# Strassen's scheme for the gate and up products of 1792 tokens: an encoder layer on one core, cut into two phases

## The chip, the core and the metric

The kernel runs on one core of one Trainium2 chip. The core has four compute engines with a queue each: TensorE (PE; PEld is its weight load), VectorE (DVE), ScalarE (ACT) and GpSimd (POOL). SyncE (SP) issues the DMA transfers. The engines run side by side and meet at semaphores. The metric is the time of one launch on the device, in microseconds (us); lower is better.

## What is computed

The reference is one layer of an encoder over 2048 prompt tokens and 32 sample tokens with state, D_MODEL = 1024:

```python
h = layer_norm(x, ln_in_g, ln_in_b)
m, states = mixer(h, ...)       # z = h @ w_in (1024 x 2304), three mixers on z, then @ w_out
h = layer_norm(ALPHA * h + m, ln1_g, ln1_b)
f = swiglu(h, w_gate, w_up, w_down)
h = layer_norm(ALPHA * h + f, ln2_g, ln2_b)

def swiglu(h, w_gate, w_up, w_down):     # 1024 x 2816, 1024 x 2816, 2816 x 1024
    a = jnp.einsum('btd,df->btf', h, w_gate)
    b = jnp.einsum('btd,df->btf', h, w_up)
    return jnp.einsum('btf,fd->btd', jax.nn.silu(a) * b, w_down)
```

The mixers are A (convolution of width 4 and a gated linear recurrence), B (retention in chunks of 64) and C (attention over a window of 128). All is float32.

## The kernel before

**Products.** Each large product of float32 values is made of three products in a reduced float32 format: every operand is split into a high and a low part, and high x high, low x high and high x low are added up in PSUM. A weight tile arrives in `stage` by DMA (`feed`, L172); ScalarE copies it to `whi` (`first_part`, L177), VectorE subtracts that from `stage` to give `wlo` (`second_part`, L182). `product` (L727) makes 24 matmuls of a unit, 3 x 8 slices of 128 of the 1024 features, the weights being the stationary side and the tokens the columns that stream. The columns of the normalized rows are held as hA (before the mixers) and hB (before the gate), high and low.

**Blocks.** The tokens are cut in blocks of 256, 384, 384, 384, 384 and 256, with the sample's 32 in the first one (288 columns). Per block there are units of four kinds:
- W: 18 units, the input projection, each 24 matmuls; results leave through ScalarE to the mixers' buffers.
- O: 8 units, the output projection. Here tokens are stationary and 512 weight columns stream (`t_unit`, L811 to L813; the sample's part L819); `accumulate` adds to the rows in `tok` (L837, L839).
- G: 44 units, gate and up of each of 22 feature tiles of 128 (`gu_unit`). Of a gate unit ScalarE takes tanh (L782) and VectorE forms silu (L783); of an up unit VectorE multiplies (L788), ScalarE copies the high part g_h (L789), VectorE subtracts for g_l (L794).
- D: the down projection of a group of feature tiles, added to the rows. The groups are tiles 0 to 5, 6 to 11, 12 to 17 and 18 to 21. A D unit holds two feature tiles; a group's products begin with its first two.

**Order.** `seq` is written out by hand: the G and D units of a block are followed by W of the block two further on, with O of the next block between its feature tiles 17 and 18. What is not a unit (the mixers, LayerNorms, transposes) runs as side threads, Python generators: before each unit `step` lets threads go on as far as a credit allows that grows by `rate` a unit (twice a unit where "twice" is set). The mixers of block b + 1 run through the G units of block b. Before each unit `feed` issues DMA loads as far as four `stage` buffers allow, and `split` has the parts of the next units made. The order in which the program calls the engines is the order on each engine's queue.

LayerNorm (`norm`) takes statistics on VectorE (L290), normalizes on ScalarE (L298), multiplies on VectorE (L300) and adds on GpSimd (L302); `to_features` transposes rows on TensorE. `last` (L1030 to L1064) ends the program token tile by token tile.

Of the kernel before, what the change touches and what calls it, by code (L numbers as in the profile page):

```python
# [15 lines left out]
D = 1024  # L16
# [16 lines left out]
START = tuple(int(x) for x in np.cumsum((0,) + BLOCKS[:-1]))  # L33
# [12 lines left out]
# Column offsets of the tables that depend on shapes alone.  # L46
# [37 lines left out]
def tile_hybrid_step(ctx: ExitStack, tc: tile.TileContext, io, outs):  # L84
# [4 lines left out]
    sb = ctx.enter_context(tc.tile_pool(name="sb", bufs=1))  # L89
    ps = ctx.enter_context(tc.tile_pool(name="ps", bufs=1, space=bass.MemoryType.PSUM))  # L90
    ctx.enter_context(tc.manual_schedule())

# [6 lines left out]
    # ---------------------------------------------------------------- blocks  # L99
    def ptok(b):  # L100
        return BLOCKS[b]

    def ncol(b):
        return BLOCKS[b] + (DEC if b == 0 else 0)

    def ttiles(b):
        t = [(i * 128, 128) for i in range(BLOCKS[b] // 128)]
        return t + ([(BLOCKS[b], DEC)] if b == 0 else [])

    # ---------------------------------------------------------------- token rows  # L110
    tok = {}

    def load_x(b, ts=(0, 1, 2)):
        for t, (c0, rows) in enumerate(ttiles(b)):
            if t not in ts:
                continue
            x = sb.tile([128, D], F32, name="tok", bufs=9)
# [4 lines left out]
            tok.setdefault(b, []).append(x)  # L122

    load_x(0, (0,))
    head = cst.tile([128, 144], F32, name="head")
    ident = head[:, :128]
    g_in, b_in = head[:, 128:136], head[:, 136:144]
    tb = cst.tile([128, TB_W], F32, name="tb")
    sm = cst.tile([128, SM_W], F32, name="sm")
# [5 lines left out]
    # Products of zeros wake the tensor engine's clock.  # L135
    busy = sb.tile([128, 512], F32, name="bc", bufs=2)
# [20 lines left out]
    # ---------------------------------------------------------------- weights  # L157
# [4 lines left out]
    def raw(u):  # L162
        """Whether the unit's own values are read by the tensor engine too."""
# [27 lines left out]
    # ---------------------------------------------------------------- side work  # L191
# [10 lines left out]
    def advance(name):  # L202
        """The thread's next stage; about how much work for the vector engine it is."""
# [9 lines left out]
    def step():  # L213
        """Some side work: a stage of each thread whose turn it is, while there is time for it."""
# [12 lines left out]
    def pipeline(gens, every):  # L227
        """Generators one after the other, each starting some stages after the last."""
# [34 lines left out]
    # ---------------------------------------------------------------- layer norms  # L263
    def bcast(name):
        t = sb.tile([128, D], F32, name="bc", bufs=2)
# [4 lines left out]
    def norm(name, b, g, be):  # L270
        """LayerNorm of the block's rows, in place."""
        while norming:
            yield
        norming.append(name)
        gt, bt = bcast(g), bcast(be)
        st = sb.tile([128, 3, 2, 6], F32, name="ln_st", bufs=2)
        mv = sb.tile([128, 3, 2], F32, name="ln_mv", bufs=2)
        rs = sb.tile([128, 3], F32, name="ln_rs", bufs=2)
# [27 lines left out]
        if name == "n1":  # L306
            # The first block's rows, of which only the columns have had them.
# [3 lines left out]
    def to_features(b, hi, lo):  # L311
        """Rows to feature-major columns, each value as two float32r parts."""
# [13 lines left out]
    def hl(b, tag):  # L326
        n = ncol(b)
        return (sb.tile([128, 8, n], F32R, name=tag + "h"), sb.tile([128, 8, n], F32R, name=tag + "l"))

    hA, hO, hB = {}, {}, {}  # L330
# [8 lines left out]
    def ln1(b):  # L339
        yield from norm(f"m{b}", b, "ln1_g", "ln1_b")  # L340

    def h1(b):
        hB[b] = hl(b, "hB")
        yield from to_features(b, *hB[b])

    def ln1_h1(b):
        yield from ln1(b)
        yield from h1(b)

    def ln2(b):  # L350
        yield from norm(f"y{b}", b, "ln2_g", "ln2_b")
        for t, (c0, rows) in enumerate(ttiles(b)):
            if c0 < BLOCKS[b]:
# [4 lines left out]
        del tok[b]  # L358

    # ---------------------------------------------------------------- persistent state of the mixers  # L360
    kb = cst.tile([128, 512], F32, name="kb")
    ks = S("ck")
    axtail = cst.tile([128, 2, 3], F32, name="axtail")
    lru = cst.tile([128, 2], F32, name="lru")
    ret = cst.tile([128, 2, 128], F32, name="ret")
    ret_s = S("ret").rearrange("p (t e) -> p t e", t=2)
    lam = cst.tile([128, 8, 2], F32, name="lam")
    hb = cst.tile([128, 2, 2], F32, name="hb")
    SBUFS = {}
    for kv in range(2):  # L370
        SBUFS["e", kv] = cst.tile([128, 2, 193], F32, name=f"sbe{kv}")
        SBUFS["o", kv] = cst.tile([128, 2, 257], F32, name=f"sbo{kv}")
# [6 lines left out]
    def prepare(b):  # L379
        """-4 and 2 softplus(-lambda), and half the gates' biases."""  # L380
# [861 lines left out]
```

## Time and profile before

| | |
|---|---|
| median of 3 runs | 2348.68 us (2348.56 to 2350.0) |
| span of the profiled execution | 2347.9 us |
| PE busy | 2319.7 us, 99%, 13755 matmuls |
| DVE busy | 1494.9 us, 64% |
| ACT busy | 1012.5 us, 43% |
| POOL busy | 283.9 us, 12% |
| DMA | 328.42 MB, 140 GB/s |

The profile is one execution recorded by the hardware. A row of the groups has line, engine, operation, output and inputs, shapes and count; then busy time in us and mean ns of one; then the idle time of the engine ahead of these instructions and the work that ended it. A row of the timeline has start and duration in us; what stands in brackets is idle time before the instruction and what ended it. A matmul's duration in the timeline contains its way through the array, so the pitch of a run of matmuls is read from start to start.

### The profile page before, as it was taken

What the parts mean: (1) busy time and instruction counts of PE and PEld (TensorE: products, weight loads), DVE (VectorE), ACT (ScalarE), POOL (GpSimd) and SP (SyncE); (2) the same over time, 40 slices, a digit from 0 to 9 for tenths busy, and PEclk for the clock granted to TensorE, in tenths of its full rate; (3) what the DMA queues carried; (4) which work ended last, traced back from release to release, by engine and by line L of the source; (5) the groups of instructions that cost most, each with busy time, mean ns of one, the idle gap of its engine ahead of it and who ended that gap; (6) DMA issues with size and microseconds to landing.
All of it is one profiled execution on the core that took longest, in us unless ns stands there. A gap on an engine that the chain in (4) does not pass through costs nothing. (4 is left out here: it accounts for less than half of the span.)

```text
span 2347.9 us, 34907 instructions
## 1 busy us (share of the span) xinstructions
PE 2319.7 (99%) x13755; PEld 2106.4 (90%) x13755; DVE 1494.9 (64%) x2401; ACT 1012.5 (43%) x1662; POOL 283.9 (12%) x321
## 2 busy tenths in 40 slices
PE   9899999999999999999999999999999999999998
PEld 7789888789988989998898999899899988989997
DVE  8666877583766548466664755666477565457656
ACT  5534555343543424444443434444344434334443
POOL 4112321031110002111000120100013000001001
PEclk9999999999999999999999999999999999999999
DMA  6225434444432334443233354233345323344654
GB/s 227 99 94 200 140 119 143 146 168 157 147 112 100 113 123 141 171 157 111 102 110 123 135 173 153 106 108 108 126 137 211 122 99 119 127 169 153 209 186 153
DMA packets 91907, 328.42 MB, mean 140 GB/s; under 512 B 11488, under 2 KB 12320, under 8 KB 91744
## 3 DMA queue, kind: packets, MB, share of 16 engines
q1 hardware_dynamic: 91744, 326.20, 40.0%
q8 instruction: 108, 1.77, 0.3%
q14 instruction: 55, 0.45, 0.1%
HBM read 317.34 MB, written 8.82 MB: 139 GB/s over the span
## 5 line engine op out<-in xcount | busy, mean ns | idle before, releaser
L182 DVE TENSOR_TENSOR wlo<-stage,whi 128x1024 fp32r<-128x1024 f32 x549 | 729.1, 1329 | 373.0 <-PE mm L813 122.7
L177 ACT ACTIVATE whi<-stage 128x1024 fp32r<-128x1024 f32 x551 | 580.7, 1054 | 446.7 <-PE mm L812 329.9
L727 PE MATMUL mm<-hBh,whi 128*128 128x384 f32 (+2 forms) x2112 | 388.5, 325 | 0.0
L727 PE MATMUL mm<-hBh,wlo 128*128 128x384 f32 (+2 forms) x2112 | 376.1, 319 | 3.9 <-DVE wlo L182 3.8
L727 PE MATMUL mm<-hBl,whi 128*128 128x384 f32 (+2 forms) x2112 | 376.1, 319 | 0.0
L727 PEld LDWEIGHTS mm<-hBh,whi 128*128 128x128 f32 x2112 | 337.5, 189 | 14.8 <-issue 8.5
L727 PEld LDWEIGHTS mm<-hBh,wlo 128*128 128x128 f32 x2112 | 341.1, 188 | 4.8 <-DVE wlo L182 4.8
L727 PEld LDWEIGHTS mm<-hBl,whi 128*128 128x128 f32 x2112 | 341.3, 188 | 0.0
L811 PE MATMUL mm<-whi,g_h 128*128 128x512 f32 x688 | 277.2, 403 | 0.1
L813 PE MATMUL mm<-wlo,g_h 128*128 128x512 f32 x688 | 272.7, 396 | 0.0
L812 PE MATMUL mm<-whi,g_l 128*128 128x512 f32 x688 | 271.3, 394 | 0.0
L789 ACT ACTIVATE g_h<-g_t 128x384 fp32r<-128x384 f32 (+2 forms) x132 | 65.4, 495 | 351.6 <-DVE g_t L788 351.6
L783 DVE SCALAR_TENSOR_TENSOR g_t<-g_t,mm 128x384 f32<-128x384 f32 (+2 forms) x132 | 67.9, 514 | 192.5 <-ACT g_t L782 191.9
L788 DVE SCALAR_TENSOR_TENSOR g_t<-g_t,mm 128x384 f32<-128x384 f32 (+2 forms) x132 | 67.9, 514 | 162.4 <-PE mm L727 162.0
L727 PE MATMUL mm<-hAh,wlo 128*128 128x384 f32 (+2 forms) x864 | 157.0, 324 | 7.0 <-DVE wlo L182 7.0
L811 PEld LDWEIGHTS mm<-whi,g_h 128*128 128x128 f32 x688 | 129.2, 188 | 38.5 <-issue 7.8
L782 ACT ACTIVATE g_t<-mm 128x384 f32<-128x384 f32 (+2 forms) x132 | 60.6, 459 | 233.6 <-PE mm L727 233.5
L727 PE MATMUL mm<-hAh,whi 128*128 128x384 f32 (+2 forms) x864 | 157.8, 324 | 1.0 <-DVE zb L939 0.5
L813 PEld LDWEIGHTS mm<-wlo,g_h 128*128 128x128 f32 x688 | 129.2, 188 | 31.5 <-DVE wlo L182 0.4
L727 PE MATMUL mm<-hAl,whi 128*128 128x384 f32 (+2 forms) x864 | 155.5, 322 | 0.0
L812 PEld LDWEIGHTS mm<-whi,g_l 128*128 128x128 f32 x688 | 129.3, 188 | 28.9
L295 POOL TENSOR_TENSOR ln_rs<-ln_rs,mhalf 128x1 f32<-128x1 f32 (+1 forms) x46 | 36.8, 799 | 944.9 <-DVE ln_mv L293 944.9
(273 smaller groups left out, 2691.1 us busy)
## 6 DMA issues: line engine op xcount, KB each, us to landing
stage<-in_wgu SPq DMA_DIRECT2D x264, 512.0 KB, 3.5
stage<-in_wdn SPq DMA_DIRECT2D x132, 512.0 KB, 3.5
stage<-in_win SPq DMA_DIRECT2D x108, 512.0 KB, 3.5
stage<-in_wout SPq DMA_DIRECT2D x48, 512.0 KB, 3.5
tok<-in_x SPq DMA_DIRECT2D x16, 512.0 KB, 6.0
out_y<-tok SPq DMA_DIRECT2D x14, 512.0 KB, 5.4
bc<-in_ln_g SPq DMA_DIRECT2D x12, 512.0 KB, 5.4
bc<-in_ln_b SPq DMA_DIRECT2D x12, 512.0 KB, 6.2
```

The lines of the kernel that those rows point to most:

```text
L177: act.activation(whi[u], staged[u], AF.Copy)
L182: eng.tensor_tensor(wlo[u], staged[u], whi[u].bitcast(F32), op=ALU.subtract)
L295: pool.tensor_tensor(rs[:rows, t:t + 1], rs[:rows, t:t + 1], mhalf[:rows, 0:1], op=ALU.pow)
L727: pe.matmul(p, w[:, k, :], a[:, k, :], start=(x == 0 and k == 0), stop=(x == 2 and k == 7))
L782: act.activation(t, p[:, :N], AF.Tanh, scale=0.5)
L783: dve.scalar_tensor_tensor(t, t, 1.0, p[:, :N], op0=ALU.add, op1=ALU.mult)
L788: dve.scalar_tensor_tensor(t, t, 0.5, p[:, :N], op0=ALU.mult, op1=ALU.mult)
L789: act.activation(gh, t, AF.Copy)
L811: pe.matmul(o, ah[:, cs], wh[:, x, :], start=first and x == 0, stop=False)
L812: pe.matmul(o, al[:, cs], wh[:, x, :], start=False, stop=False)
L813: pe.matmul(o, ah[:, cs], wl[:, x, :], start=False, stop=last and x == 1)
```

## The change

The program falls into two phases.

**Phase 1** has W and O of all blocks, the mixers and the first two LayerNorms, and the whole SwiGLU of block 0 alone (at its end, groups of four feature tiles). W of block b + 1 is followed by O of block b; the mixers of a block run beside the W and O units of its neighbours, with rate 1.8 and two steps a unit. The rows after the second LayerNorm go to DRAM, and so do their transposes (`to_memory`, instead of the split into hB).

**Phase 2** has the SwiGLU of the other 1792 tokens. Phase 1's buffers in SBUF and PSUM are given up and new ones opened in their place. The tokens form two parts of 896, each of two halves of 448. In a part, for each feature tile, gate and up form a product of a 2 x 2 block matrix of the columns (halves of tokens by halves of features, 448 x 512) with a 2 x 2 block matrix of the weights (halves of features by gate and up). Strassen's scheme, in Winograd's form, makes it of 7 block products for 8, each of 3 x 4 matmuls of 448 columns. The operands are sums of blocks: those of the columns are made once a part (`columns`: 14 copies on ScalarE, 14 subtractions and 8 sums of 896 on VectorE), those of the weights for every feature tile (sums on GpSimd, copies on ScalarE, subtractions on VectorE, tiles of 512). The gate and up values are sums of products, formed by `after_p1` to `after_p3` when a product leaves PSUM.

Weight work is a list of jobs, of which `background(3)` does up to three behind each product; seven pairs of high and low parts and six unsplit tiles are held. `down` is the down projection of a group of three (twice two) feature tiles over the seven token tiles of the part; `finale` the last one with the last LayerNorm.

```diff
-GROUPS = ((0, 6), (6, 12), (12, 18), (18, 22))
+GROUPS0 = ((0, 4), (4, 8), (8, 12), (12, 16), (16, 20), (20, 22))
+GROUPSS = ((0, 3), (3, 6), (6, 9), (9, 12), (12, 15), (15, 17), (17, 19), (19, 22))
+HALF = 448
+PART = 2 * HALF
+NPAIR = 7
+NRAW = 6
...
+    phase.close()
+    phase = ctx.enter_context(ExitStack())
+    sb = phase.enter_context(tc.tile_pool(name="ff", bufs=1))
+    ps = phase.enter_context(tc.tile_pool(name="pf", bufs=1, space=bass.MemoryType.PSUM))
...
+            for x, th, kh in (("a", 0, 0), ("d", 0, 1), ("c", 1, 1), ("b", 1, 0)):
+                w[x] = two()
+                sp.dma_start(w[x], cols1[s, th, kh][:, k, :])
...
+        def multiply(n, left, right, first):
+            if first:
+                bank[n] = gbank()
+            (wl, wh), = need([(s, f, right)])
+            xl, xh = X[left]
+            for x, (w, a) in enumerate(((wh, xh), (wl, xh), (wh, xl))):
+                for k in range(4):
+                    pe.matmul(bank[n], w[:, k * 128:k * 128 + 128], a[:, k, :],
+                              start=first and x == 0 and k == 0,
+                              stop=x == 2 and k == 3, skip_group_check=not first)
+            drop([(s, f, right)])
...
+        def after_p3():
+            t = GT[f] = sb.tile([128, 2, PART], F32R, name="g", bufs=3)
+            dve.tensor_tensor(v["u2"], v["u2"], bank["z"], op=ALU.add)
+            dve.scalar_tensor_tensor(v["u2"], v["g1"], 0.5, v["u2"], op0=ALU.mult, op1=ALU.mult)
+            dve.scalar_tensor_tensor(v["g2"], v["g2"], 1.0, v["c"], op0=ALU.add, op1=ALU.mult)
+            act.activation(t[:, 1, :HALF], v["u2"], AF.Copy)
+            dve.scalar_tensor_tensor(v["p5"], v["g2"], 0.5, v["p5"], op0=ALU.mult, op1=ALU.mult)
+            act.activation(t[:, 1, HALF:], v["p5"], AF.Copy)
+
+        def low():
+            t = GT[f]
+            dve.tensor_tensor(t[:, 0, :], v["raw"].rearrange("p a b -> p (a b)"), t[:, 1, :].bitcast(F32),
+                              op=ALU.subtract)
...
+        for n, left, right, first, then in (
+                ("x", "a11", "b11", True, after_p1), ("z", "s1", "t1", True, after_p5),
+                ("y", "s2", "t2", True, after_p6), ("x", "a12", "b21", False, after_p2),
+                ("v", "a22", "t4", True, after_p4), ("y", "s3", "t3", False, after_p7),
+                ("z", "s4", "b22", False, after_p3)):
+            multiply(n, left, right, first)
+            catch_up()
+            behind(then)
+            background(3)
+            step()
+        behind(low)
...
+    def down(s, g, more=None):
+
+        fs = list(range(*GROUPSS[g]))
+        catch_up()
+        for half in range(2):
+            need([(s, f, half) for f in fs])
+            banks_ = {}
+            if half == 0:
+                for t in range(2):
+                    banks_[t] = dbank()
+                    d_part(s, half, t, fs[:-1], banks_[t], True, False)
```

`catch_up` calls what `behind` put off, so a product's results leave PSUM behind the next product; before `down`, those of the last product of a group are called ahead of its matmuls.

Three places in the queues. On SP before, in the middle of the program, weight loads wait only for the buffer that they overwrite (`in_wdn` is the down weights, `in_wgu` gate and up; the bracket names the engine or DMA queue waited for):

```order
L172 DMA stage<-in_wdn 128x1024 [waits DMAHW1_49,DVE_49]
L172 DMA stage<-in_wgu 128x1024 [waits DMAHW2_49,DVE_49,Activation_49]
L172 DMA stage<-in_wgu 128x1024 [waits DMAHW3_49,DVE_49]
L172 DMA stage<-in_wgu 128x1024 [waits DMAHW4_49,DVE_49]
L172 DMA stage<-in_wgu 128x1024 [waits DMAHW5_49,DVE_49]
```

On SP now, where phase 1 ends (`stage` is its last weights) and phase 2 begins (`ww` its weight tiles, `cols` the columns in DRAM):

```order
L206 DMA stage<-in_wdn 128x1024 [waits DMAHW2_49,PE_49]
L206 DMA stage<-in_wdn 128x1024 [waits DMAHW4_49,DVE_49]
L1190 DMA ww<-in_wgu 128x512 [waits DMAHW5_49,DMAHW0_49,DMAHW6_49,DVE_49,DMAHW7_49,PE_49,Pool_49]
L1190 DMA ww<-in_wgu 128x512 x5
L1153 DMA two<-cols_75 128x896
L1153 DMA two<-cols_76 128x896
L1153 DMA two<-cols_78 128x896 [waits DMAHW1_49]
```

The first load of phase 2 waits for every engine, for TensorE's last product among them (L909), and all loads behind it stand in the same queue.

On TensorE before, where the down products of a group follow on its last gate and up unit (mm is a bank of PSUM, g_h and g_l the parts of a feature tile's result):

```order
L727 MATMUL mm<-hBh,whi 128x384 x7
L727 MATMUL mm<-hBh,wlo 128x384 x8
L727 MATMUL mm<-hBl,whi 128x384 x8
L811 MATMUL mm<-whi,g_h 128x512 [waits Activation_49]
L812 MATMUL mm<-whi,g_l 128x512
L813 MATMUL mm<-wlo,g_h 128x512 [waits DVE_49]
```

And now, the end of a group's last seventh product, the products of the tiles that are ready, and the first of the last tile (gu and dn are banks, g both parts of a result):

```order
L1323 MATMUL gu<-xh,wl 128x448 x4
L1323 MATMUL gu<-xl,wh 128x448 x4
L1386 MATMUL dn<-wh,g 128x512
L1387 MATMUL dn<-wh,g 128x512
L1388 MATMUL dn<-wl,g 128x512
...
L1386 MATMUL dn<-wh,g 128x512 [waits Activation_49]
L1387 MATMUL dn<-wh,g 128x512 [waits DVE_49]
L1388 MATMUL dn<-wl,g 128x512
```

The waits of the down products stood behind the first two of six tiles' weights; they stand now behind 12 matmuls of the last tile's two neighbours, and wait for that last tile. On VectorE, at the same place, now:

```order
L1351 TENSOR_TENSOR two<-two,gu 128x448 [waits DVE_49,PE_49]
L1352 TENSOR_TENSOR two<-two,gu 128x448 [waits DVE_49]
L1203 TENSOR_TENSOR wl<-ww,wh 128x512 [waits DMAHW1_49,Activation_49]
L1358 TENSOR_TENSOR two<-two,gu 128x448 [waits PE_49]
L1359 SCALAR_TENSOR_TENSOR two<-two 128x448 [waits DVE_49]
L1360 SCALAR_TENSOR_TENSOR two<-two 128x448
L1362 SCALAR_TENSOR_TENSOR two<-two 128x448 [waits DVE_49,Pool_49]
L1367 TENSOR_TENSOR g<-two,g 128x896 [waits Activation_49]
L1393 SCALAR_TENSOR_TENSOR tok<-tok,dn 128x512 [waits DMAHW0_49,PE_49]
```

A weight's subtraction (L1203, waiting for ScalarE's copy) stands ahead of the four operations on the seventh product and of the subtraction that gives the low part (L1367).

More of the change, by code (lines that the diff above doesn't have):

```diff
@@ L785, in gu_unit @@
             t = gate_bank.pop(f)
-            gh = sb.tile([128, N], F32R, name="g_h", bufs=6)
-            gl = sb.tile([128, N], F32R, name="g_l", bufs=6)
+            f0, f1 = next(g for g in GROUPS0 if g[0] <= f < g[1])
+            if f == f0:
+                g_parts[0] = hl(b, "hC", 4, 2)
+            gh, gl = (x[:, f - f0, :] for x in g_parts[0])
             dve.scalar_tensor_tensor(t, t, 0.5, p[:, :N], op0=ALU.mult, op1=ALU.mult)
@@ new lines, in weights_d, with loads @@
+    def weights_d(s, g, half):
+        f0, f1 = GROUPSS[g]
+        for f in range(f0, f1):
+            w_load((s, f, half), io["wdn"][half * (FT // 2) + f // 2][:, (f % 2) * 512:(f % 2) * 512 + 512])
+        for f in range(f0, f1):
+            w_hi((s, f, half), (s, f, half))
+            w_lo((s, f, half), (s, f, half), True)
+    def loads():
+        while clock["next"] < len(jobs) and (jobs[clock["next"]][0] != "load" or clock["raw"] < NRAW):
+            kind, fn, _ = jobs[clock["next"]]
+            if kind == "load":
+                fn()
+            clock["next"] += 1
@@ new lines, in job, with background @@
+    def job():
+        kind, fn, _ = jobs[clock["done"]]
+        if kind == "pair" and clock["pairs"] == NPAIR:
+            return False
+        if kind != "load":
+            fn()
+        clock["done"] += 1
+        return True
+    def background(n):
+        clock["slot"] += 1
+        loads()
+        while n and clock["done"] < clock["next"]:
+            kind, _, on = jobs[clock["done"]]
+            if any(landed.get(k, 0) > clock["slot"] for k in on) or not job():
+                break
+            n -= kind != "load"
@@ new lines, in need, with drop @@
+    def need(keys):
+        for k in keys:
+            while clock["done"] <= ends[k]:
+                loads()
+                assert clock["done"] < clock["next"] and job(), k
+        return [pairs[k] for k in keys]
+    def drop(keys):
+        for k in keys:
+            del pairs[k]
+            clock["pairs"] -= 1
+    ends = {}
+    for s_ in range(NPART):
+        for g_, (f0_, f1_) in enumerate(GROUPSS):
+            for f_ in range(f0_, f1_):
+                weights_gu(s_, f_)
+            for half_ in range(2):
+                weights_d(s_, g_, half_)
@@ new lines, in d_part, with d_add @@
+    def d_part(s, half, t, fs, bank, first, last):
+        for f in fs:
+            wl, wh = pairs[s, f, half]
+            gl, gh = (GT[f][:, i, t * 128:t * 128 + 128] for i in range(2))
+            pe.matmul(bank, gh, wh, start=first and f == fs[0], stop=False)
+            pe.matmul(bank, gl, wh, start=False, stop=False)
+            pe.matmul(bank, gh, wl, start=False, stop=last and f == fs[-1])
+    def d_add(s, half, t, bank, fresh):
+        r = tok[NBLK + s][t][:, half * 512:half * 512 + 512]
+        if fresh:
+            dve.scalar_tensor_tensor(r, r, ALPHA, bank, op0=ALU.mult, op1=ALU.add)
+        else:
+            dve.tensor_tensor(r, r, bank, op=ALU.add)
@@ new lines, in down @@
+    def down(s, g, more=None):
[8 more added lines that the diff above has]
+                    d_part(s, half, t, fs[:-1], banks_[t], True, False)
+            for t in range(PART // 128):
+                if t in banks_:
+                    d_part(s, half, t, fs[-1:], banks_[t], False, True)
+                else:
+                    banks_[t] = dbank()
+                    d_part(s, half, t, fs, banks_[t], True, True)
+                catch_up()
+                behind(lambda t=t, b=banks_[t], half=half: d_add(s, half, t, b, g == 0))
+                if more:
+                    next(more, None)
+                background(3)
+                step()
+            drop([(s, f, half) for f in fs])
@@ new lines, in finale @@
+        normal(t, c2)
+        whole(t, c0)
+        affine(t, c2, pool, pool)
+        whole(t, c1)
+    pace.update(rate=1.0, credit=0.0, twice=False)
+    start("y0", ln2(0))
+    loads()
+    for _ in columns(0):
+        background(2)
+    for s_ in range(NPART):
+        for g_, (f0_, f1_) in enumerate(GROUPSS):
+            for f_ in range(f0_, f1_):
+                gu(s_, f_)
+            if g_ == 0:
+                drain("y0" if s_ == 0 else f"y{NBLK + s_ - 1}")
+            if g_ < len(GROUPSS) - 1:
+                down(s_, g_)
+            elif s_ < NPART - 1:
+                more_ = columns(s_ + 1)
+                down(s_, g_, more_)
+                catch_up()
+                for _ in more_:
+                    pass
+                start(f"y{NBLK + s_}", ln2(NBLK + s_))
+            else:
+                finale(s_, g_)
```

553 lines of the change are left out of this document (368 added, 185 removed).

## The prediction

> **What bounds the kernel now.** I read the head of the page first, then the waits of TensorE, then the timeline for the pitch of its products.
>
> ```profile
> span 2347.9 us, 34907 instructions
> PE 2319.7 (99%) x13755; PEld 2106.4 (90%) x13755; DVE 1494.9 (64%) x2401; ACT 1012.5 (43%) x1662; POOL 283.9 (12%) x321
> PEclk9999999999999999999999999999999999999999
> ```
>
> ```profile
> engine line waited for: us in total, times, longest us
> PE mm L727 <- DVE wlo L182: 10.9, 6, 6.3
> PE mm L919 <- ACT tok L914: 2.6, 2, 1.9
> ```
>
> TensorE is busy 99% of the span and its longest class of waits is 10.9 us. So the time is the number of matmuls times their pitch, and two things can move it: fewer columns to stream, or TensorE made to wait where it does not wait now.
>
> The pitch is read from where one product's group of eight starts to where the next starts (the columns are start, duration, line, tile):
>
> ```profile
> 1001.69 1.55 PE L727 MATMUL mm<-hAl,whi 128*128 128x384 f32 x8
> 1003.07 1.55 PE L727 MATMUL mm<-hAh,whi 128*128 128x384 f32 x8
> ...
> 2203.66 1.12 PE L727 MATMUL mm<-hBh,whi 128*128 128x256 f32 x8
> 2204.62 1.12 PE L727 MATMUL mm<-hBh,wlo 128*128 128x256 f32 x8
> ...
> 2330.18 0.40 PE L1030 MATMUL mm<-whi,g_h 128*128 128x512 f32 x1
> ...
> 2331.81 0.39 PE L1031 MATMUL mm<-hAh,g_l 128*128 128x512 f32 x1
> ```
>
> With the rest of the timeline (8 to a row, and 7 between the last two) that is 1.387/8 = 173 ns for 384 columns, 0.963/8 = 120 ns for 256 and 1.63/7 = 233 ns for 512.
>
> **The change, part by part.** The sum is made against the profiled span, 2347.9 us; the median of the runs is 2348.7, 0.8 above it, and I leave that difference alone.
>
> *Gate and up products.* Before, the 1792 tokens behind block 0 take 44 units of 24 matmuls in each of four blocks of 384 and one of 256: 4224 x 0.1734 + 1056 x 0.120 = 732 + 127 = 859 us. After, 22 feature tiles x 2 parts x 7 products x 12 = 3696 matmuls of 448. No row has 448: per column 384 gives 202 ns, 512 gives 204; I take 203. 3696 x 0.203 = 750 us, so **-109 us** (-105 to -112). Down, output and input products and block 0 keep their matmuls, so this is the whole gain. All else is waiting.
>
> The costs need the durations of the other engines:
>
> ```profile
> L182 DVE TENSOR_TENSOR wlo<-stage,whi 128x1024 fp32r<-128x1024 f32 x549 | 729.1, 1329 | 373.0 <-PE mm L813 122.7 <-PE mm L727 118.4 <-issue 101.8
> L839 DVE TENSOR_TENSOR tok<-tok,mm 128x512 f32<-128x512 f32 x92 | 63.2, 688 | 40.5 <-PE mm L813 39.9
> L290 DVE BATCH_NORM_STATS2 ln_st<-tok 128x6 f32<-128x512 f32 x88 | 56.2, 680 | 0.0
> L783 DVE SCALAR_TENSOR_TENSOR g_t<-g_t,mm 128x384 f32<-128x384 f32 x88 | 48.7, 554 | 150.6 <-ACT g_t L782 150.0
> L789 ACT ACTIVATE g_h<-g_t 128x384 fp32r<-128x384 f32 x88 | 46.3, 526 | 259.5 <-DVE g_t L788 259.5
> L319 ACT ACTIVATE hBh<-sd 128x512 fp32r<-128x512 f32 x30 | 15.9, 587 | 0.1
> L302 POOL TENSOR_TENSOR tok<-tok,bc 128x1024 f32<-128x1024 f32 x44 | 110.6, 2515 | 198.4 <-DVE tok L300 197.1 <-DVE lam L396 1.3
> ```
>
> Between these shapes I interpolate: VectorE 0.62 us for 448 and 1.10 for 896 (between 0.688 at 512 and 1.23 for an L182 that runs alone, quoted below), ScalarE 0.57 for 448 and 0.59 for 512, GpSimd half of 2.5 for 512, 1.26.
>
> *The step between the phases.* The first weight and column loads of phase 2 stand on SP's queue behind a wait for the last product of phase 1 (the new pools reuse its memory), so nothing of phase 2 is prepared while phase 1 computes. A load of this size takes, from issue to landing (last column, us):
>
> ```profile
> stage<-in_wgu SPq DMA_DIRECT2D x264, 512.0 KB, 3.5
> ```
>
> Six weight loads of 256 KB and four of 0.46 MB come at once: 3.4 MB against 3.5 us for half a MB; I estimate 7 us (4 to 11) until VectorE has its first operands. It then has, in its order up to the operand of the seventh product, 22 operations of 896 and 8 of 512: 22 x 1.10 + 8 x 0.69 = 30 us, less some 2 for overlap at their ends. ScalarE's 14 + 8 copies (about 18 us) run beside it. The seventh product (12 x 0.203 = 2.4 us) follows, and ends at 7 + 28 + 2.4 = 37 us, where TensorE's own work is 84 x 0.203 = 17: 20 us too late. Loads of the second slice wait for buffers, and GpSimd's sums interfere (below), for which I choose 10 more: **+30 us** (18 to 42). And TensorE is cold after that:
>
> ```profile
> 64.56 2.29 PE L727 MATMUL mm<-hAh,wlo 128*128 128x288 f32 x8 [6.32 <-DVE wlo L182]
> 66.64 2.12 PE L727 MATMUL mm<-hAl,whi 128*128 128x288 f32 x8
> ...
> 70.05 1.34 PE L727 MATMUL mm<-hAh,whi 128*128 128x288 f32 x8
> 71.23 1.21 PE L727 MATMUL mm<-hAh,wlo 128*128 128x288 f32 x8
> ```
>
> After a wait of 6.32 us eight matmuls of 288 took 2.08 us, a little later 1.18: some 4 us at about half speed, so **+2 us**. The Trainium skill, "TensorE: Matmul & The Clock Gate", section "What's actually happening", says that the clock is halved after an idle window of some 3.4 us and restored after a busy one; these rows agree. That page speaks against each shorter wait below as well, if it passes that length; this is a rival.
>
> *Entry into the down products.* Before, the last gate product's chain is hidden under down products of other feature tiles. After, a group has only 3 tiles (2 in two of the eight groups), and its products start with the tiles that are ready (6 or 12 matmuls of 512 for two token tiles), then need the last tile. Its chain hangs on the seventh product: the scalar copy of a weight into the buffer that this product releases and VectorE's subtraction of it stand ahead in the two queues (0.59 + 0.69), then four operations of 448 (2.48), a copy (0.57), a subtraction of 896 (1.10), and hand-offs. From a product's end to the start of the vector operation, and from there to ScalarE's copy:
>
> ```profile
> 2326.50 0.39 PE L1030 MATMUL mm<-whi,g_h 128*128 128x512 f32 x1
> ...
> 2326.70 0.42 DVE L788 SCALAR_TENSOR_TENSOR g_t<-g_t,mm 128x256 f32<-128x256 f32 x1 [0.84 <-PE mm L727]
> ...
> 2327.16 0.42 ACT L789 ACTIVATE g_h<-g_t 128x256 fp32r<-128x256 f32 x1 [1.94 <-DVE g_t L788]
> ```
>
> it is 0.20 us, counted from when the next product begins; and 2326.70 + 0.42 to 2327.16 is 0.04; with 0.04 for each of four hand-offs, 5.8 us in all. Cover is 13 matmuls (3.0 us) or 7 (1.6), so TensorE waits 2.8 or 4.2 us: 11 x 2.8 + 4 x 4.2 + 4.2 for the last group = **+52 us** (25 to 68; without the weight's pair ahead it is 1.28 less each time, some 32, and one more operation ahead gives 16 more).
>
> *Where part 0 ends.* The second part's columns are made between the last down products of the first: VectorE then has 22 x 1.10 + 14 x 0.69 for residuals and 6 x 0.69 for weights = 38 us, TensorE 126 x 0.233 = 29, but the columns of the later products have another 17 us of gate products to come in: **+7** (0 to 14).
>
> *The end.* Each of the last seven token tiles takes 18 x 0.233 = 4.2 us of TensorE and on VectorE two additions (1.38), four statistics of 256 (1.7 by half of L290 and an overhead), two multiplications (1.38) and half a us of small ones: 5.0. 7 x 0.8 = **+6** (3 to 13).
>
> *Phase 1.* The mixers of a block, spread before over input, output, gate and down products, now run beside input and output products alone:
>
> ```profile
> 50.00:150.00 100.00, 91.95 (x635) 83.70 (x634) 71.73 (x169) 51.83 (x118) 16.80 (x21) 0.97 0.29 97
> 150.00:350.00 200.00, 199.07 (x1330) 172.31 (x1328) 146.53 (x252) 100.32 (x172) 46.77 (x47) 1.00 0.42 147
> 1040.00:1400.00 360.00, 360.00 (x1983) 325.60 (x1982) 223.70 (x349) 149.99 (x244) 37.78 (x42) 1.00 0.36 125
> ```
>
> The columns are stretch, length, then busy time (and count) of PE, PEld, DVE, ACT and POOL, and the granted clock. VectorE is 62% busy at 1040 to 1400, 73% at 150 to 350. Counting its operations in the new order by these durations gives 77 to 88 us a block beside some 95 to 115 of TensorE, about 80%. At 73% TensorE lost under 1 us in 200; in the prologue, where mixers already run so beside input products, it lost 8 in 100. Five blocks of some 105 us between these two: **+13** (-5 to 42; a gain only from side products that now fall into waits that stand there anyway).
>
> *GpSimd's sums.* Each feature tile has four weight sums and one sum of products on GpSimd, 5 x about 1.26 us, which the kernel before does not have. These rows show what that does to a vector operation with two operands in SBUF:
>
> ```profile
> 203.81 2.40 POOL L302 TENSOR_TENSOR tok<-tok,bc 128x1024 f32<-128x1024 f32 x1 [2.30 <-DVE tok L300]
> 204.99 2.29 DVE L182 TENSOR_TENSOR wlo<-stage,whi 128x1024 fp32r<-128x1024 f32 x1 [1.26 <-ACT tok L298]
> ...
> 213.31 1.23 DVE L182 TENSOR_TENSOR wlo<-stage,whi 128x1024 fp32r<-128x1024 f32 x1 [1.35 <-PE mm L727]
> ```
>
> The subtraction, 1.23 alone, takes 2.29 and ends 1.07 after GpSimd's: it stood until GpSimd was done. The Trainium skill, "SBUF — State Buffer", section "Who interferes with whom", has the two engines share a port pair under an exclusive lock; the rows agree. In a feature tile's 17 us VectorE has 7 x 0.69 + 8 x 0.62 + 1.10 = 11 us; five full blockings would make it 17. Half of that is likelier, since GpSimd's sums meet other operations too. Weights are split several products ahead and results have two banks' time, which covers a blocking here and there: **+6** (0 to 44, a us per tile, if not).
>
> Sum: 2347.9 - 109 + 32 + 52 + 7 + 6 + 13 + 6 = 2355 us.
>
> **The rivals.** *The waits are cheap* (0.27). Phase 1 goes as 150 to 350 went, at no cost, the boundary and the end cost 4 each, the sums nothing, and the entries lose only what lies without the weight's pair ahead, 32: 2347.9 - 109 + 32 + 32 + 8 = 2311 us, faster. For it: TensorE's 199.07 of 200 at 73%. Against it: the weight's copy waits for the very product that starts the chain. It decides if an entry costs under 2 us.
>
> *VectorE binds phase 1* (0.16). Each of the five blocks loses as the prologue did and as much again when threads must be finished: 9 us x 5 = 45 instead of 13, 2387 us. For it: 91.95 of 100. Against it: 6.3 us of that were one wait. It decides if VectorE is over 90% busy there.
>
> *The entries cool the clock* (0.05): if each of 15 waits of 3 to 4 us brings the half speed seen after 6.32, 2 us each, 2385 us. Against it: they are shorter than the wait shown.
>
> *The lock binds phase 2* (0.04): a us in each of 44 tiles instead of 6 in all, 2393 us.
>
> *The change doesn't do what it says* (0.02): if matmuls of 448 took the 233 ns of 512, 3696 x 0.233 = 861 us and the gain is gone, 2355 + 111 = 2466 us.
>
> **How the numbers follow.** The forecast has 0.46, with its own range of 2338 to 2372; the measurement can tell about 0.2%, 2344 to 2353.4. Of the 0.46 I put 0.12 below that, 0.15 inside, 0.19 above. Faster: 0.27 + 0.12 = 0.39; same 0.15; slower 0.19 + 0.16 + 0.05 + 0.04 + 0.02 = 0.46. The range of 8 in 10 begins at 2311, which leaves half of the first rival (0.13) out, and ends at 2400, which leaves the last rival and some 0.05 of the others out.
>
> **What would show it.** Right: one wait of TensorE of some 25 to 40 us in all around the step between the phases, with PEclk down after it; 15 waits of 2.5 to 4.5 us ending at VectorE's subtraction of 896 (L1367); matmuls of 448 at 203 ns; phase 1 with VectorE near 80% and TensorE's losses under 30 us. Wrong: entries under 1.5 us, or waits spread evenly through phase 2 at weights (L1203) or evacuations, or phase 1 longer by more than 45 us than its matmuls.

## The result, and the profile after

The changed kernel takes 2537.24 us (median of 4 runs, 2535.89 to 2537.74) against 2348.66 us for the kernel before: a ratio of 1.0801, with a 95% interval of 1.0786 to 1.0817. The forecast was 2355 us, with a range of 2311 to 2400.

The head of the page of the changed kernel:

```profile
span 2535.7 us, 32439 instructions
PE 2303.7 (91%) x12168; PEld 1995.3 (79%) x12168; DVE 1618.6 (64%) x2703; ACT 975.4 (38%) x1808; POOL 575.5 (23%) x541
PEclk9999999999989999987999999999989999999998
```

TensorE has 1587 matmuls fewer, yet it is busy only 16 us less than before, and idle for 232 us of the span instead of 28. So there are two losses: waits, and matmuls that take longer. Where TensorE waits, longest first:

```profile
engine line waited for: us in total, times, longest us
PE dn L1387 <- DVE g L1367: 40.5, 15, 4.7
PE dn L1386 <- ACT g L1361: 39.8, 15, 4.7
PE gu L1323 <- ACT xh L1143: 20.4, 2, 19.2
PE sd L646 <- DVE b_o L641: 17.2, 4, 10.3
PE gu L1323 <- ACT two L1331: 16.7, 3, 8.7
PE mm L815 <- DVE wlo L216: 12.9, 4, 6.3
PE gu L1323 <- ACT wh L1198: 12.7, 1, 12.7
```

The first two rows are the 15 entries into down products (80 us); L1143, L1198 belong to the step between the phases, L646 and L815 to phase 1, L1331 mostly to the part boundary. The same program in six stretches: phase 1, the step with the first three feature tiles, part 0, the part boundary, part 1, the end (columns: stretch, length, busy time and count of PE, PEld, DVE, ACT, POOL, then the granted clock):

```profile
0.00:1122.90 1122.90, 1056.70 (x6615) 919.55 (x6615) 796.39 (x1513) 564.20 (x1103) 232.16 (x270) 0.97 0.43 141
1122.90:1231.70 108.80, 62.15 (x261) 53.66 (x253) 72.09 (x94) 39.30 (x59) 31.74 (x24) 0.78 0.39 134
1231.70:1836.20 604.50, 562.24 (x2522) 486.34 (x2521) 338.71 (x480) 174.09 (x305) 127.56 (x100) 0.96 0.18 60
1836.20:1949.70 113.50, 89.08 (x380) 75.25 (x379) 80.45 (x116) 34.42 (x55) 44.95 (x36) 0.89 0.30 110
1949.70:2482.50 532.80, 501.43 (x2270) 435.91 (x2269) 287.27 (x418) 153.63 (x277) 114.91 (x91) 0.96 0.16 55
2482.50:2535.70 53.20, 32.06 (x136) 24.64 (x134) 43.72 (x86) 9.79 (x10) 24.13 (x22) 0.85 0.19 69
```

The clock is 0.96 to 0.97 in the long parts, where the kernel before had 1.00 (rows of 150 to 350 and 1040 to 1400 us in the prediction). Set beside the terms of the forecast, each worked out from the starts of matmuls (length of a stretch less its matmuls at 203.5 ns for 448 columns and 231.5 ns for 512):

| term | forecast us | measured us |
|---|---|---|
| gate and up, matmuls at full pace | -109 | 752.1 - 859 = -107 |
| step between the phases | +32 | gap 13.1 + first stretch 44.5 = +58 |
| entries into the down products | +52 | 524.2 - 398.6 = +126 |
| part boundary, gate products | +7 | +22 |
| the end | +6 | 53.2 - 27.1 - 11.4 of the kernel before = +15 |
| phase 1 | +13 | 1122.9 - 1052 for the same work before = +71 |
| rest of the gate products | +6 | +4 |
| sum (the spans differ by 188) | +7 | +189 |

The 1052 is the span before less 859 for gate and up, 1839 x 0.2315 for the down products of the same tokens up to the end, and the same 11.4 us at the end.

**One entry.** The timeline of the changed kernel where the first group's down products begin:

```profile
1231.70 0.39 PE L1386 MATMUL dn<-wh,g 128*128 128x512 f32 x1
...
1232.11 0.58 ACT L1354 ACTIVATE two<-two 128x448 f32<-128x448 f32 x1 [2.01 <-DVE two L1352]
...
1232.59 0.62 ACT L1198 ACTIVATE wh<-ww 128x512 fp32r<-128x512 f32 x1
...
1233.24 0.69 DVE L1203 TENSOR_TENSOR wl<-ww,wh 128x512 fp32r<-128x512 f32 x1 [1.23 <-ACT wh L1198]
...
1233.85 0.61 DVE L1358 TENSOR_TENSOR two<-two,gu 128x448 f32<-128x448 f32 x1
1234.01 2.89 POOL L1211 TENSOR_TENSOR ww<-ww 128x512 f32<-128x512 f32 x2 [1.35 <-DVE wl L1203]
...
1234.50 1.28 DVE L1359 SCALAR_TENSOR_TENSOR two<-two 128x448 f32<-128x448 f32 x1
1235.70 1.69 DVE L1360 SCALAR_TENSOR_TENSOR two<-two 128x448 f32<-128x448 f32 x1
...
1236.44 0.50 PE L1386 MATMUL dn<-wh,g 128*128 128x512 f32 x1 [1.78 <-ACT g L1361]
1237.49 0.62 DVE L1362 SCALAR_TENSOR_TENSOR two<-two 128x448 f32<-128x448 f32 x1
...
1238.76 1.09 DVE L1367 TENSOR_TENSOR g<-two,g 128x896 fp32r<-128x896 f32 x1 [0.64 <-ACT g L1363]
1239.90 0.80 PE L1387 MATMUL dn<-wh,g 128*128 128x512 f32 x1 [2.96 <-DVE g L1367]
1240.49 0.63 PE L1388 MATMUL dn<-wl,g 128*128 128x512 f32 x1
1240.92 0.63 PE L1386 MATMUL dn<-wh,g 128*128 128x512 f32 x1
```

Three things are to be seen. The weight pair (L1198, L1203) stands ahead of L1358, as forecast. Its subtraction then releases two sums on GpSimd (L1211), and while these run L1359 and L1360 take 1.28 and 1.69 us instead of 0.62: together 1.73 us of standing still. And behind 4.7 us of waits the matmuls of 512 start 0.43 us apart (1240.49 to 1240.92), where 0.23 is the pace.

### The profile page after: what moved, and what is told of

It reads as the page before. It is cut to its first block, busy times and chain, and to the rows that moved or that the text cites. A ratio compares the mean times of both kernels' runs of the same rounds, so it can differ in the third digit from the quotient of the medians.

```text
span 2535.7 us, 32439 instructions
## 1 busy us (share of the span) xinstructions
PE 2303.7 (91%) x12168; PEld 1995.3 (79%) x12168; DVE 1618.6 (64%) x2703; ACT 975.4 (38%) x1808; POOL 575.5 (23%) x541
## 5 line engine op out<-in xcount | busy, mean ns | idle before, releaser
L1203 DVE TENSOR_TENSOR wl<-ww,wh 128x512 fp32r<-128x512 f32 x396 | 297.5, 763 | 297.9 <-ACT wh L1198 296.7
L1198 ACT ACTIVATE wh<-ww 128x512 fp32r<-128x512 f32 x396 | 242.6, 625 | 609.3 <-PE dn L1387 295.4
L1211 POOL TENSOR_TENSOR ww<-ww 128x512 f32<-128x512 f32 x176 | 233.2, 1325 | 803.7 <-DVE wl L1203 641.3
L216 DVE TENSOR_TENSOR wlo<-stage,whi 128x1024 fp32r<-128x1024 f32 x221 | 285.3, 1291 | 142.2 <-issue 56.9
L1323 PE MATMUL gu<-xh,wh 128*128 128x448 f32 x1232 | 308.9, 373 | 59.7 <-ACT xh L1143 20.4
L1323 PE MATMUL gu<-xl,wh 128*128 128x448 f32 x1232 | 305.3, 370 | 3.5 <-DVE xl L1146 3.5
L1323 PE MATMUL gu<-xh,wl 128*128 128x448 f32 x1232 | 306.4, 371 | 0.0
L211 ACT ACTIVATE whi<-stage 128x1024 fp32r<-128x1024 f32 x222 | 233.9, 1054 | 151.7 <-PE mm L902 69.4
L1387 PE MATMUL dn<-wh,g 128*128 128x512 f32 x574 | 243.0, 423 | 40.5 <-DVE g L1367 40.5
L1386 PE MATMUL dn<-wh,g 128*128 128x512 f32 x574 | 240.9, 420 | 41.1 <-ACT g L1361 39.8
L1323 PEld LDWEIGHTS gu<-xh,wl 128*128 128x128 f32 x1232 | 235.0, 191 | 21.2
L1388 PE MATMUL dn<-wl,g 128*128 128x512 f32 x574 | 239.3, 417 | 0.0
L815 PE MATMUL mm<-hAh,wlo 128*128 128x384 f32 (+2 forms) x1216 | 224.4, 329 | 12.9 <-DVE wlo L216 12.9
L815 PE MATMUL mm<-hAh,whi 128*128 128x384 f32 (+2 forms) x1216 | 220.7, 324 | 1.0 <-DVE zb L1024 0.5
L815 PE MATMUL mm<-hAl,whi 128*128 128x384 f32 (+2 forms) x1216 | 212.4, 318 | 0.0
L815 PEld LDWEIGHTS mm<-hAh,wlo 128*128 128x128 f32 x1216 | 195.3, 197 | 21.4 <-DVE wlo L216 13.9
L815 PEld LDWEIGHTS mm<-hAh,whi 128*128 128x128 f32 x1216 | 188.7, 191 | 14.2 <-issue 9.3
L815 PEld LDWEIGHTS mm<-hAl,whi 128*128 128x128 f32 x1216 | 194.1, 194 | 0.0
```

The source lines that it names most:

```text
L211: act.activation(whi[u], staged[u], AF.Copy)
L216: eng.tensor_tensor(wlo[u], staged[u], whi[u].bitcast(F32), op=ALU.subtract)
L815: pe.matmul(p, w[:, k, :], a[:, k, :], start=(x == 0 and k == 0), stop=(x == 2 and k == 7))
L1198: act.activation(pairs[key][1], whole_w[x], AF.Copy)
L1203: dve.tensor_tensor(pairs[key][0], whole_w[x], pairs[key][1].bitcast(F32), op=ALU.subtract)
L1211: pool.tensor_tensor(whole_w[x], whole_w[a], whole_w[b], op=ALU.subtract)
```

## The experiments

The theory after this reading: the chain into the down products is lengthened by the weight pair and by GpSimd's sums, and the wait that results halves the clock; in phase 1, VectorE has too much to do where mixers and LayerNorms meet, GpSimd's additions included. The rival for the entries: the serial chain alone makes the wait. The rival for phase 1: the order of the threads. Each run has one time, beside 2348 to 2349 us of the kernel before on the same chip; only differences of 10 us and more are read from it.

**No weight jobs at the entry.**

```diff
-            background(3)
+            background(0 if end and n == "z" and not first else 3)
```

> Behind the last product of a group no weight job is done (15 places), so neither a weight's copy and subtraction nor GpSimd's sums lie beside the chain into the down products. Theory (the chain is delayed by the pair, 1.3 us, and by GpSimd's sums that block VectorE, 1.7 us; the wait is then long enough to halve the clock, some 2.5 us more): down stretches of 126 matmuls fall from about 37 to about 31.5 us, 15 x 6 = 90 us less, 2446 us in all, and no half clock behind an entry. Rival (the chain's own eight steps are the wait, GpSimd and the clock play no part): only the pair's 1.3 us go, 15 x 1.3 = 20 us, 2516 us.

Measured: 2473.04 us, 64 less. The same place in its timeline:

```profile
1233.11 0.62 DVE L1359 SCALAR_TENSOR_TENSOR two<-two 128x448 f32<-128x448 f32 x1
...
1233.65 0.62 DVE L1360 SCALAR_TENSOR_TENSOR two<-two 128x448 f32<-128x448 f32 x1
...
1236.79 0.50 PE L1387 MATMUL dn<-wh,g 128*128 128x512 f32 x1 [1.37 <-DVE g L1367]
1237.13 0.39 PE L1388 MATMUL dn<-wl,g 128*128 128x512 f32 x1
1237.35 0.40 PE L1386 MATMUL dn<-wh,g 128*128 128x512 f32 x1
```

Both operations take 0.62 again, the wait is 1.37, and the matmuls behind it start 0.23 apart. A stretch of 126 down matmuls in part 0 falls from between 36 and 37.4 us to 31.0. Two-tile entries still lose 6.7 to 7.7 us, and the two entries beside the part boundary 5.6 and 8.5, which is why 64 and not 90 us went. The rival's 20 us are refuted.

**The pair stays, the sums go behind the chain.** The jobs at the place are cut to two, and the next sums run on VectorE (`dve` for `pool` in `w_sum`) behind the chain.

> The weight pair stays ahead of the chain, but the two sums that ran on GpSimd beside it are done by VectorE behind the chain. Theory (lock): VectorE's two operations of 448 there fall from 1.28 and 1.69 to 0.62 us, the chain ends 1.7 us earlier, 26 us less in all, and up to 63 us less where the wait becomes too short to halve the clock: 2473 to 2510 us. Rival (no lock): the operations stay as long, no gain, and two operations of 0.69 more on VectorE: 2536 us or some more.

Measured: 2499.74 us, 37.5 less, with most stretches of 126 at 34.4 us. L1359 and L1360 take 0.63 and 0.62 us at the first entry, and from the start of the products behind it to the end of L1367 it is 6.46 us instead of 8.15: 1.7 us at each of 15 entries would be 25 us of the gain. So taking GpSimd's sums away gives over half of what the first run gave. The clock is only in part behind this: it still falls at eight of the nine three-tile entries that do not lie beside the part boundary, where TensorE waits 1.2 and then 1.9 us.

**TensorE kept busy.** First with 12 matmuls that nobody reads, then with ten more inside the remaining wait:

```diff
+                spare_work(s, half, fs[0], 12 if len(fs) == 3 else 20)
...
+            if fill:
+                spare_work(s, half, f, fill)
```

> Twelve matmuls of 448 columns, which nobody reads, stand between the covering products and the last tile's at 15 entries (2.4 us of work each, inside a wait of 5 us). Theory (the wait halves the clock): TensorE is idle for under 3 us, the matmuls behind stay at 0.23 us, some 2.5 us less at each three-tile entry, 25 to 38 us in all, 2500 to 2510 us. Rival (the matmuls behind an entry are slow for another reason): no gain, 2536 us, or more by what the added matmuls don't hide.

> As the run with filling matmuls, which still left an idle stretch of 2.7 us behind which the matmuls ran at half speed; ten more matmuls that nobody reads stand between the last tile's first product and its second, and 20 for 12 ahead at two-tile entries. TensorE is idle for well under 1.5 us at each entry. Theory (the clock falls after an idle stretch between 1.4 and 2.7 us): no half speed behind the entries, 15 x 2.4 us less, about 2500 us. Rival (the slow matmuls come from something that the entry does, whatever TensorE did before): they stay slow, 2525 us.

Measured: 2524.75 and 2510.4 us, 12.5 and 27 less. The first fell short of its forecast. At its first entry:

```profile
1238.26 0.58 PE L1387 MATMUL dn<-wh,g 128*128 128x512 f32 x1 [2.66 <-DVE g L1367]
1238.64 0.63 PE L1388 MATMUL dn<-wl,g 128*128 128x512 f32 x1
1239.07 0.63 PE L1386 MATMUL dn<-wh,g 128*128 128x512 f32 x1
```

An idle stretch of 2.66 us was left, and the matmuls behind it start 0.43 us apart. At the fourth entry of the same run they do not:

```profile
1499.59 0.50 PE L1387 MATMUL dn<-wh,g 128*128 128x512 f32 x1 [2.58 <-DVE g L1367]
1499.92 0.39 PE L1388 MATMUL dn<-wl,g 128*128 128x512 f32 x1
1500.16 0.39 PE L1386 MATMUL dn<-wh,g 128*128 128x512 f32 x1
```

Behind the same 2.58 us at the fifth entry they are at 0.43 again. Of nine such entries, all with a wait of 2.58 to 2.66 us, the clock fell at five and stayed at four, so the length of the idle stretch does not decide alone. The clock records of the 15 traces of this case show what goes with it: the granted clock changes only at points a multiple of 3.41 us apart. Of the intervals between two neighbouring points that ran at full clock, all 316 in which TensorE was busy for less than 43% (as the profile counts it) were followed by half clock, 54 of the 332 between 43% and 73%, and none of the 9449 above. At these nine entries the clock fell where 2.09 us or more of the wait lay in one interval, and stayed where a point parted it into pieces of 1.74 us or less.

In the second run:

```profile
1240.20 0.50 PE L1395 MATMUL dn<-wh,g 128*128 128x512 f32 x1 [0.55 <-DVE g L1367]
1240.54 0.39 PE L1396 MATMUL dn<-wl,g 128*128 128x512 f32 x1
1240.77 0.39 PE L1392 MATMUL dn<-wh,g 128*128 128x512 f32 x1
```

The chain ends as late as before (the product waits until 1240.20), but the matmuls behind run at 0.23 us: the slow matmuls come from the idle time, not from the work around them, and they are worth some 27 us. The forecast of about 2500 us was not reached.

**The low part by halves**, besides no jobs at the entry:

```diff
+            dve.tensor_tensor(t[:, 0, :HALF], v["u2"], t[:, 1, :HALF].bitcast(F32), op=ALU.subtract)
...
-            dve.tensor_tensor(t[:, 0, :], v["raw"].rearrange("p a b -> p (a b)"), t[:, 1, :].bitcast(F32),
-                              op=ALU.subtract)
+            dve.tensor_tensor(t[:, 0, HALF:], v["p5"], t[:, 1, HALF:].bitcast(F32), op=ALU.subtract)
```

> As the run without jobs at the entry, and the low part of a group's last tile is made by halves of 448, the first half right behind its copy. Theory (what is left of the wait is the serial chain): the first half's parts are there some 2.6 us after the seventh product, inside the 12 covering matmuls (2.8 us), so three-tile entries cost about 0 instead of 1.9 and two-tile entries about 1.3, too short to halve the clock, instead of 6.7: 42 us less than without jobs alone, 2430 us. Rival (the entry waits for something that the chain does not contain, a bank or a weight): little changes, 2460 to 2473 us.

Measured: 2447.79 us. Stretches of 126 in part 0 are 29.3 us, their matmuls alone 29.2: three-tile entries are free. Two-tile ones keep 3.8 to 6.0 us and those beside the part boundary 5.7 and 11.6, so 25 and not 42 us went.

**Eight plain products in phase 2.** No scheme, no sums; phases, groups and down products as in the changed kernel.

> Phase 2 without Strassen's scheme: the two phases, the columns through memory, the groups and the down products stay, but gate and up are eight products of the plain blocks (no sums on VectorE or GpSimd, silu as before). TensorE has 528 matmuls of 448 more, +107 us. Theory (the scheme brings its waits: the chain behind the seventh product, GpSimd's sums, the sums of columns): the entries cost some 15 us instead of 126, the step between the phases and the part boundary some 45 less: 2537 + 107 - 110 - 45 = 2490 us, so two phases alone are some 140 us slower than the kernel before. Rival (the waits belong to two phases and small groups, whatever the scheme): 2537 + 107 = 2620 to 2644 us.

Measured: 2459.81 us, 77 *less* than with the scheme, though TensorE has 107 us more of matmuls. From the second group to the part boundary (columns as above):

```profile
1200.40:1788.90 588.50, 588.50 (x2749) 516.39 (x2749) 229.94 (x353) 123.36 (x205) 0.00 (x0) 1.00 0.19 62
```

TensorE waits nowhere in 588.5 us and GpSimd does nothing. All down stretches together are 402.0 us where 398.6 is the pace; the first stretch loses 12.7 instead of 44.5, the part boundary nothing. The rival (waits belong to phases and groups) is refuted for phase 2: its waits came with the scheme, that is with its sums and with seven weight blocks to split for four. Those of phase 1 stay (it ends 5 us earlier, at 1117.4), and with them the two phases without the scheme are 111 us slower than the kernel before.

**Early columns.**

```diff
+        for x, th, kh in (("a", 0, 0), ("d", 0, 1), ("c", 1, 1), ("b", 1, 0)):
+            ahead[x] = row_tile()[:, :2 * HALF].rearrange("p (k c) -> p k c", c=HALF)
+            sp.dma_start(ahead[x], cols1[0, th, kh][:, 0:2, :])
```

> Half of the first part's columns are loaded into row buffers during the end of phase 1, the other half at the start of phase 2, so no column load waits for a buffer. Theory (about 10 us of the 57 at the step are loads): the first column operation starts with the phase and the first three tiles' products end 10 to 14 us earlier, 2523 to 2527 us. Rival (VectorE's 30 operations in their order are all that counts): under 4 us, 2533 us or more.

Measured: 2526.88 us, 10.4 less: the gap behind phase 1 falls from 13.1 to 3.7 us, the first stretch keeps its 44.3. So loads are 10 of the 58 us there. The first stretch is not made longer by them; with eight products, which need no sums, it lost 12.7, so the scheme's work on the operands makes most of it.

**LayerNorm's additions on VectorE** (`dve` for `pool` in two lines).

> The last addition of every LayerNorm goes from GpSimd (2.4 us each, 1024 wide) to VectorE. Theory (in phase 1 and at the part boundary VectorE stands still behind these additions): the waits of TensorE in phase 1, 62 us now, fall by half, and the boundary by some 10 us: 2490 to 2500 us. Rival (VectorE is simply full there): 1.2 us more vector work for each of some 55 tiles makes the waits longer, 2550 to 2580 us.

Measured: 2509.59 us, 28 less. Phase 1 ends 24.4 us earlier (1098.5); the part boundary gains 1 us, not 10. VectorE's busy time in phase 1 falls from 796 to 783 us although it now does the additions as well. How an addition on GpSimd delays it is seen ahead of the worst wait of the changed kernel's phase 1:

```profile
739.67 2.34 POOL L337 TENSOR_TENSOR tok<-tok 128x1024 f32<-128x1024 f32 x1 [2.04 <-DVE tok L335]
740.18 2.92 DVE L216 TENSOR_TENSOR wlo<-stage,whi 128x1024 fp32r<-128x1024 f32 x1
743.02 1.09 DVE L641 TENSOR_SCALAR b_o<-sd,b_mv,b_rs 128x64 f32<-128x64 f32 x4
743.75 0.89 PE L646 MATMUL sd<-head,b_o 128*128 128x128 f32 x2 [10.28 <-DVE b_o L641]
```

The subtraction L216, 1.22 alone, takes 2.92 beside the addition and ends 1.09 behind it, and L641, for which TensorE has waited 10 us, stands in the queue behind. Most of those 10 us have other causes, for this wait hardly shrinks when the additions move; the weights' subtractions gain more, L815 falling from the 12.9 us shown above. The run's rows for the two:

```profile
PE sd L646 <- DVE b_o L641: 15.2, 3, 9.7
PE mm L815 <- DVE wlo L216: 7.2, 4, 2.8
```

**The threads' credit.**

> The side threads of phase 1 get a credit of 2.6 a step for 1.8, nothing else changes. Theory (the mixers' last stages are called in a burst when a block's threads must be finished, and TensorE waits in the burst): with more credit less is left for the burst, the waits of phase 1 (62 us) fall by some 20 us, 2515 us. Rival (VectorE has no room beside input and output products, whenever the stages are called): the waits only move, 2530 to 2545 us.

> The side threads of phase 1 get a credit of 1.3 a step for 1.8. Theory (VectorE's operations stand in the queue ahead of the weights' subtractions and the mixers' own chains, and a larger credit lets more of them in at once, which cost 15 us at 2.6): a smaller credit spreads them, 5 to 15 us less, 2522 to 2532 us. Rival (1.8 lies between both evils: at 1.3 the rest is called in bursts where threads must be finished): 2545 us or more.

Measured: 2552.17 us with 2.6 and 2597.57 with 1.3, against 2537 with 1.8. With 2.6 phase 1 ends 16 us later, with 1.3 59 us later. Neither direction helps, and the theory that I gave for each run failed. At 2.6 the time lies past the rival's 2545 us too; at 1.3 the rival came true, and 1.8 lies between the two evils. Another order of the threads was not tried.

**Bare norms.**

> Left out: the multiplication and the addition of scale and shift in the LayerNorms of phase 1 (31 tiles of 1024), so VectorE has 38 us less work there and GpSimd's additions are gone too; the order of all else is kept. Theory (VectorE's load where norms and mixers meet makes the waits): phase 1 gains clearly more than the 24 us that moving the additions gave, 40 us or more, 2497 us or less. Rival (the additions on GpSimd were all, the rest is chains between TensorE and VectorE in the order of the threads): 24 to 28 us, 2509 to 2513 us.

Measured: 2476.17 us, 61 less. Phase 1 ends at 1065.7, 57 us earlier, where moving the additions gave 24. The largest wait of phase 1 is then (first rows of TensorE's waits up to 1080 us, the first being the step between the phases):

```profile
PE gu L1324 <- ACT wh L1199: 13.7, 1, 13.7
PE sd L647 <- DVE b_o L642: 8.0, 3, 4.1
PE mm L1005 <- ACT tok L1000: 3.1, 2, 2.3
```

So 57 of the 71 us of phase 1 go with the norms' multiplications and additions, in the same order of threads. Moving the additions from GpSimd gave 24 of them; the other 33 lie between a phase 1 that has both operations on VectorE and one that has neither. It is VectorE's load where norms and mixers meet, with GpSimd's additions as a part of it, at an average of only 71% busy (796 of 1123 us).

**The mends together, with and without the scheme.** No jobs at the entry, halves, early columns, additions on VectorE; and, for the eight products, the last two of these.

> The mends together: no jobs at the entry, low parts by halves, early columns, the LayerNorms' additions on VectorE. Theory (their causes are separate): the gains add up from the run with halves, 2447.8 - 28 - 10 = 2410 us, so the kernel stays some 60 us behind the one before, by phase 1, the step and the part boundary. Rival (they share a cause, VectorE's time): under half of the 38 us, 2430 us or more.

> Eight plain products with early columns and the LayerNorms' additions on VectorE. Theory (phase 1 gains the same 23 us as in the other program, the step less, since it is shorter): 2459.8 - 23 - 6 = 2431 us; against 2410 us with the mended scheme, seven products for eight bring 21 us of the 107. Rival (the additions cost as much on VectorE where GpSimd has no sums): 2450 us or more, and the scheme brings 40 us.

Measured: 2416.13 and 2431.6 us. The gains add up to within 6 us, and seven products for eight bring 15.5 us of the 107. No version beat the kernel before.

## Why the prediction was wrong

**The bound and the pitch held.** TensorE's matmuls at full pace fell by 107 us where 109 were forecast, and 448 columns take 203.5 ns between starts where 203 was interpolated.

**The step that failed first: "entry into the down products", +52, measured +126.** The chain was put at 5.8 us with the weight pair in it. From the start of the products behind it to the end of L1367 it is 8.15 us (1231.70 to 1239.85): 1.73 more by GpSimd's sums and some 0.6 mostly because ScalarE's tanh (L1354) precedes the pair's copy, which starts 0.89 after those products instead of 0.20. The lock was in the prediction, with its price from the right rows, but I set it against the steady products, where it costs next to nothing (+4 with all else), and into the 10 us chosen for the step, and not against the one chain for which TensorE waits. Then the clock: I gave the rival "the entries cool the clock" 0.05 because the waits were shorter than the 6.32 us for which a row showed it. They are shorter, 4.7 us in two pieces, and halve the clock all the same; that rival's price of 2 us each, 30 in all, is close to the 27 measured. The Trainium skill, "TensorE: Matmul & The Clock Gate", section "What's actually happening", speaks of an idle window of some 3.4 us. The 3.41 us between the points of change agree with that length, but TensorE was never idle for a whole one where 2.58 us sufficed, and the measurement decides.

Three runs split the 126: filling the waits gave 27 (the clock), taking pair and sums away gave 64 with most of the clock in it, halving the low part 25 more. The 38 us that are left lie at the two-tile entries and the two beside the part boundary.

**Phase 1, +13, measured +71.** I took an average share of VectorE (80%) between two stretches of the kernel before and read off a loss. What counted was not the average, which came out at 71%, but stretches in which norms and mixers stand in one queue ahead of what TensorE needs. Bare norms give 57 us back; that the rest, 14 us, is near the 13 that I had forecast for the whole is chance. The second rival ("VectorE binds phase 1", 0.16) named this place, at 45 us, and asked for over 90% busy: the place was right and the sign to look for wrong, for no stretch of 100 us between 100 and 900 us shows more than 79%. The sign that I set for being wrong, a phase 1 longer by over 45 us, came.

**The step between the phases, +32, measured +58.** The loads were 10 us where 7 were estimated; VectorE's operations, what they wait for and the cold clock came to 47 where 25 were put. Beside GpSimd's sums single ones are doubled:

```profile
1136.85 3.98 POOL L1211 TENSOR_TENSOR ww<-ww 128x512 f32<-128x512 f32 x2 [19.50 <-DVE wl L1203]
1137.66 2.04 DVE L1149 TENSOR_TENSOR two<-two 128x896 f32<-128x896 f32 x1
1139.62 2.15 DVE L1146 TENSOR_TENSOR xl<-two,xh 128x896 fp32r<-128x896 f32 x1
```

L1149 and L1146 are 1.08 alone. How the rest divides between the lock, the order of the operations and the half clock (0.78 in that stretch) was not tried apart.

**The part boundary, +7, measured +22**, and the end, +6, measured +15: the same kind of term, too small as I take it for the same reason. With eight products the boundary costs under 2 us, so the scheme brings it. That it is the sums of columns and weights together with the second LayerNorm is my reading and was not tried apart; moving that one's additions to VectorE did not help. The end was not tried.

**The first rival** (waits cheap, 2311 us) is refuted as the kernel stands, though three-tile entries can be made free, as the run with halves shows.

## What to carry to other kernels

A scheme that saves matmuls pays in sums and in more parts to split, and both fall on the engines between which operands are handed over: here seven products for eight saved 107 us of TensorE, and cost 184 in waits and half clock against eight plain products in the same frame. Cost such a change at the places where a chain of several engines is as long as TensorE's cover, count there what stands ahead in each queue *and* what GpSimd does beside VectorE, and then ask whether the wait, with other idle time within 3.4 us of it, is long enough to halve the clock. Where such a wait can't be removed, filling it with matmuls that nobody reads kept the clock up here. An average share of VectorE says little about a phase in which several threads meet: look for the stretch where they do.

## What the hardware showed that was not expected

The clock falls after short idle times, and the same idle time does not always do it: behind 2.58 to 2.66 us, five of nine entries of one run had 3.4 us at half pace (0.43 us for 512 columns instead of 0.23) and four had none. What counted was how much of an interval of 3.41 us, at fixed points of the trace, TensorE was busy: under 43% was always followed by half clock, over 73% never, and between them it was now one, now the other. The waits of 1.4 us at the three-tile entries of the run without jobs, away from the part boundary, never brought it. GpSimd's operations were stretched too: two sums of 512 took 2.89 us beside vector operations and 3.98 at the step between the phases, where the shortest single one of the run takes 1.25. The lock that the Trainium skill, "SBUF — State Buffer", section "Who interferes with whom", describes thus delays both sides; these rows agree. A vector operation of 0.62 us lost 1.07 us to it at the entry shown above, more than its own length.
